# Another order of the q, k and gate projections, and a last norm whose root comes straight from the sum of squares

## The chip, the cores and the metric

The kernel runs on one core of one Trainium2 chip. The metric is the device time of one execution in microseconds. TensorE (PE, with PEld for its weight loads) does the matmuls, VectorE (DVE) and ScalarE (ACT) the elementwise work, and SyncE's queue (SP) issues nearly all transfers.

## The reference

One layer of a hybrid encoder block on x of 1024 tokens by 1024 channels, in float32:

```python
h = x + 0.5 * SwiGLU_1(rmsnorm(x))                   # d_ff 2816
u = rmsnorm(h)
q, k, v, g_ret, p, gates = split(u @ w_in)           # 4 x 1024, 1024, 2048 columns
q = rotary(q); k = rotary(k) / 16                    # 4 heads of 256
ret = rmsnorm(retention(q, k, v)) * silu(g_ret)      # chunks of 64, decay per head
pool_out = pool_scale * (pool(p) @ pool_w)           # trailing means over 2, 4, 8, 16 tokens, minus p
gate = sigmoid(gates + gate_bias)
h = h + (gate[0] * (ret @ w_ret_up) + gate[1] * (pool_out @ w_pool_up)) @ w_out
h = h + 0.5 * SwiGLU_2(rmsnorm(h))
return rmsnorm(h)
```

## The kernel before

The stages follow one another: first feed-forward, the projections out of the second norm, retention with the pooled branch as filler between its units, the merge, the second feed-forward, and the last norm. Every float32 operand is split into a high and a low part, and a product is three matmuls (`mm3`, lines 178 to 180). A large product is a Strassen form with seven products instead of eight, so sums of weight blocks and of result blocks are made on DVE and ACT.

`projections()` runs `values()` for v and then 24 groups of 256 output channels: p0 to p3, the eight gate groups t0 to t7, and q, k, g for four heads each. `pairs()` takes two groups of the list `order` at a time. In a pair, the product P3 (`A[5]`, `B[5]`) is formed for both groups in common, by a second Strassen level of 42 matmuls of 256 columns in place of 2 x 12 of 512; after the first `some` pairs (the number that `pairs` gets) P2 is done in common in the same way, and in the first `some` pairs P2 is run for each group by itself (`A[4]`, `B[4]`).

What follows a group is set by its kind in `end()`: a q or k group is rotated on DVE (`rotate`, with the tables cos and sin made by the first rotation) and stored; a t group goes through a sigmoid on ACT with a bias column, a g group through a silu on ACT, both then stored; a p group goes through `window`, which doubles trailing sums (line 1203) on DVE, finishes the mean and stores it. These pieces are put in the queue `flow.back`. In the projections one of them is taken off after each step of seven products (`flow.rate = 1`), so what a pair leaves behind is done beside the matmuls of the next one.

A result has the tiles A and B of a group (q3A and q3B of q3). They come from a pool of nine tiles of 128x1024 (`t4`), which also holds the window sums and cos and sin; a tile is free again when the store that reads it has landed. Raw weights come in four tiles (k3ra, k3rb of k3), split weights (k3wL, k3wS) in five. PSUM has eight banks; a bank is free when DVE or ACT has emptied it. In the common product the copies at lines 563, 566 and 583 empty banks into A of one of the two groups.

Retention works in units (head, half of the tokens). A unit's q, k, v are loaded, scores s are made, scaled by the decay (sc), split (sm), k is scaled (kd) and the state st is formed. `pool(n)` is the filler: it loads the pooled tiles (pl) and the pool weight (pw), splits them and runs eight groups of three matmuls into px, which ACT and DVE empty and split into po.

At the end, `Last` is the final norm. `gains` loads its gain row (n4row), and for each of four blocks of tokens `finish` takes the sum of squares of the second half of the row (n4q), adds what is known of the first half (n4e, `self.sums`), refines one over the root by one Newton step, and scales both halves.

Of the kernel before, what the change touches and what calls it, by code (L numbers as in the profile page):

```python
# [13 lines left out]
AF = mybir.ActivationFunctionType  # L14
ALU = mybir.AluOpType
ADD, SUB, MUL = ALU.add, ALU.subtract, ALU.mult
# [3 lines left out]
D = 1024  # L20
# [30 lines left out]
N_MV, N_T4, N_RAW, N_WT, N_TL, N_C2 = 28, 9, 4, 5, 4, 8  # L51
# [39 lines left out]
def block_kernel(ctx: ExitStack, tc, x, x_tok, vecs, f1_in, f1_out, w_in, w_v, pool_w, w_ret, w_pool, w_o,  # L91
                 f2_in, f2_out, g_row, rope, decay, consts, out, out_tok):
    nc = tc.nc
    mm = nc.tensor.matmul
    tt = nc.vector.tensor_tensor
    stt = nc.vector.scalar_tensor_tensor
    act = nc.scalar.activation
# [34 lines left out]
    def sum_bank(name):  # L132

        return ps.tile([P, H], F32, tag="sum", bufs=N_SUM, name=name)

    def load(dst, src):
        nc.sync.dma_start(dst, src)

    def eights(name):

        return sb.tile([P, 32], F32, tag="ss", bufs=2, name=name)[:, :8]
# [4 lines left out]
    def half(t, j):  # L146
        return t[:, j * H : (j + 1) * H]
# [49 lines left out]
    for n in range(N_SUM):  # L197
        b = sum_bank(f"set{n}")
# [68 lines left out]
    class Next(Norm):  # L267
# [22 lines left out]
        def g(self, mt, v=None):  # L290
            if self.gain is None:
                return None
            v = vec if v is None else v
            return v[:, self.gain + mt : self.gain + mt + 1]
# [297 lines left out]
    def pairs(nx, groups, some, tags, last):  # L592

        groups = list(groups)
        for n in range(0, len(groups), 2):
            both = n >= 2 * some
            A, B = (g((2, 3) if both else (3,)) for g in groups[n : n + 2])
            yield A[0]
            yield then(B[0], last) if n == len(groups) - 2 else B[0]
            if not both:  # L600
                yield A[4]
                yield then(B[4], nx.blocks("R21", tags, True)) if n == 2 * some - 2 else B[4]
            yield from (A[3], A[1], B[3], B[1], A[2], B[2])
            yield from common(nx, A, B, 2 if both else 3)
            yield A[6]
            yield B[6]
            if both:
                yield from common(nx, A, B, 3)

    def then(step, work):  # L610


        def body():
            step[1]()
            flow.add(*work)

        return step[0], body
# [484 lines left out]
    mix = Next("n2", V_MIX, h1)  # L1102
# [230 lines left out]
        yield from product("L12", "R21", "b", True, result(0, 0, lambda i: p1s.pop(i)))  # L1333
        yield from product("L22", "T4", "a", False, result(1, 0))

    order = [o for n, p in enumerate((1, 3, 2, 0)) for o in (("p", p), ("t", n))]
    order += [o for n in range(2) for kind in "qk" for o in ((kind, n), ("t", 4 + 2 * n + "qk".index(kind)))]
    order += [("q", 2), ("k", 2), ("q", 3), ("g", 0), ("k", 3), ("g", 1), ("g", 2), ("g", 3)]

    def projections():  # L1340
        yield from values()
        flow.rate = 1
        yield from pairs(mix, (project(*o) for o in order), 4, [("tl", N_TL), ("t4", N_T4), ("t4", N_T4)],
                         [units[0].loads])
        flow.rate = 2

# [76 lines left out]
    class Unit:  # L1423
# [141 lines left out]
        def finish(self):  # L1565
            for i in range(2):
                await_stored(f"g{self.h}")
                g = tl(f"rg{self.h}{i}")
                load(g, gs[2 * self.h + i])
                for nh in range(2):  # L1570
                    b = bank(f"ot{self.h}{nh}{i}")
                    for t in range(4):
                        o = t * HD + i * P
                        nc.tensor.transpose(b[:, t * P : (t + 1) * P], self.O[nh][:, o : o + P], ident)
                    tt(half(g, nh), b, half(g, nh), MUL)
                load(ret[2 * self.h + i], g)
# [153 lines left out]
    class Last(Norm):  # L1730
# [15 lines left out]
        def turned(self, acc):  # L1746


            def gains():
                self.row = sb.tile([P, S], F32, tag="mv", bufs=N_MV, name=f"{self.name}row")  # L1750
                load(self.row, g_row)
                self.ssq_e = eights(f"{self.name}sse")

            def done(n):

                o = self.rows[n] = sb.tile([P, S], F32, tag="mv", bufs=N_MV, name=f"{self.name}o{n}")
                b = self.turn([acc[mt] for mt in range(4)], n)
                act(half(o, 1), b, AF.Square, accum_out=self.ssq_e[:, n : n + 1])
                tt(half(o, 0), b, half(self.row, 0), MUL)
                v = self.sums[n] = sb.tile([P, 8], F32, tag="st", bufs=10, name=f"{self.name}e{n}")[:, :1]  # L1760
                nc.vector.tensor_scalar(v, self.ssq_e[:, n : n + 1], 1.0 / D, EPS, MUL, ADD)

            def rest(n):

                b = self.turn([acc[mt] for mt in range(4, 8)], n)
                if n < N_SUM:
                    self.banks[n] = sum_bank(f"{self.name}s{n}")
                    copy(self.banks[n], b)
                else:
                    copy(half(self.rows[n], 1), b)  # L1770

            return gains, *(lambda f=f, n=n: f(n) for n in range(4) for f in (done, rest))
# [9 lines left out]
        def finish(self, n):  # L1782
            o, b = self.rows[n], self.banks[n]

            def st(k):
                return sb.tile([P, 8], F32, tag="st", bufs=10, name=f"{self.name}{k}{n}")[:, :1]

            ss, v, r0, r1, t = st("q"), st("v"), st("r0"), st("r1"), st("t")
            with soon():
                act(half(o, 1), b, AF.Square, accum_out=ss)  # L1790
                nc.vector.tensor_scalar(v, ss, 1.0 / D, self.sums[n], MUL, ADD)
                r = self.root(v, r0, r1, t)
                stt(half(o, 1), b, r, half(self.row, 1), MUL, MUL)
                act(half(o, 0), half(o, 0), AF.Copy, scale=r)
                nc.scalar.dma_start(out_tok[n, :, :H], half(o, 0))
                load(out_tok[n, :, H:], half(o, 1))

        def root(self, v, r0, r1, t):

            act(r0, v, AF.Sqrt)  # L1800
            nc.vector.reciprocal(r1, r0)
            tt(t, r1, v, MUL)
            stt(t, t, -0.5, r1, MUL, MUL)
            stt(r0, t, 1.5, r1, ADD, MUL)
            return r0

        def end(self, part):
            if part != 3:
# [17 lines left out]
    def second():  # L1826
        for n, step in enumerate(ffn_in(ffn2, f2_in, ops2, "c")):
            flow.rate = 1
            yield step
        flow.rate = 2  # L1830
    flow.run(chain(ffn1(), projections(), retention(), merge(), second(),
                   ffn_out(ffn2, ops2, ops_done.setdefault("c", set()), f2_out, h2, "d", fin.quarter, fin.end, fin)))
    flow.some(-1)
# [86 lines left out]
```

## Time and profile before

| | us |
|---|---|
| median of 3 runs | 2155.76 (2154.02 to 2157.71) |
| profiled execution, own time | 2155.91 |
| its span, first to last instruction | 2154.1 |
| TensorE busy | 2138.4 (99%) |
| DVE busy | 1888.1 (88%) |
| ACT busy | 1109.4 (52%) |
| granted TensorE clock, mean | 0.999 |

The time is that of the profiled execution or of the runs; the span leaves out what lies before the first and after the last instruction. A busy share of an engine is a mean over stages. DMA rows give the time from a transfer's issue to its landing.

### The profile page before, as it was taken

How to read it: one execution, taken by the hardware profiler on the slowest of the kernel's cores; microseconds unless marked ns; L12 is line 12 of the kernel's file. 1: busy time of each engine (PE TensorE's matmuls, PEld its weight loads, DVE VectorE, ACT ScalarE, POOL GpSimd, SP SyncE). 2: the span in 40 equal slices, each digit the busy share in tenths (PEclk: the TensorE clock that was granted, in tenths of full speed). 3: DMA queues.
4: the chain of work that ended last, by engine and by line, in shares of the span. 5: the costliest groups of instructions: out<-in, count | busy, mean ns of one | idle time of the engine just before them, and what ended most of it. 6: DMA issues, size and time to landing. Idle time of an engine off the chain costs nothing.

```text
span 2154.1 us, 30246 instructions
## 1 busy us (share of the span) xinstructions
PE 2138.4 (99%) x10848; PEld 1816.3 (84%) x10848; DVE 1888.1 (88%) x3358; ACT 1109.4 (52%) x2106; POOL 0.2 (0%) x4
## 2 busy tenths in 40 slices
PE   9999999999999999999999999999999999999998
PEld 7888888888887888888888898887888888888887
DVE  8798888997987799999999877899988878899796
ACT  8544444454653544545456754446644544445454
POOL 0000000000000000000000000000000000000000
PEclk9999999999999999999999999999999999999999
DMA  7232423585537233332336567634123232358642
GB/s 256 76 133 74 138 83 128 181 289 180 185 117 241 89 118 116 120 137 98 108 119 234 179 221 259 219 97 158 68 97 123 74 132 90 127 181 292 197 131 99
DMA packets 120135, 320.96 MB, mean 149 GB/s; under 512 B 13232, under 2 KB 17456, under 8 KB 119984
## 3 DMA queue, kind: packets, MB, share of 16 engines
q1 hardware_dynamic: 119408, 317.98, 43.3%
q8 instruction: 85, 1.39, 0.3%
q10 hardware_dynamic: 576, 1.05, 0.1%
q14 instruction: 66, 0.54, 0.1%
HBM read 228.27 MB, written 90.70 MB: 148 GB/s over the span
## 4 chain that ended last, share of the span: by engine, by line
PE 87%; DVE 8%; DMA 2%; ACT 2%; issue 1%; SPq 0%; DVEq 0%; ACTq 0%
PE c_b L178 2%; PE c_b L180 2%; PE c_b L179 2%; PE a_b L178 2%; PE a_b L179 2%; PE a_b L180 2%; PE c_e L178 2%; PE c_e L179 2%; PE c_e L180 2%; PE a_e L179 2%; PE a_e L178 2%; PE a_e L180 2%; PE a_a L178 1%; PE a_a L179 1%; PE a_a L180 1%; PE c_a L179 1%
## 5 line engine op out<-in xcount | busy, mean ns | idle before, releaser
L179 PE MATMUL c_b<-n3T,c_wS 128*128 128x512 f32 x176 | 68.5, 389 | 0.0
L180 PE MATMUL c_b<-n3T,c_wS 128*128 128x512 f32 x176 | 68.5, 389 | 0.0
L178 PE MATMUL c_b<-n3T,c_wS 128*128 128x512 f32 x176 | 68.2, 389 | 0.0
L178 PE MATMUL a_b<-n1T,a_wS 128*128 128x512 f32 x168 | 65.4, 389 | 0.0
L179 PE MATMUL a_b<-n1T,a_wS 128*128 128x512 f32 x168 | 65.4, 389 | 0.0
L180 PE MATMUL a_b<-n1T,a_wS 128*128 128x512 f32 x168 | 65.3, 389 | 0.0
L179 PE MATMUL a_a<-n1R,a_wL 128*128 128x512 f32 x120 | 46.7, 389 | 0.0
L178 PE MATMUL a_a<-n1R,a_wL 128*128 128x512 f32 x120 | 46.7, 389 | 0.0
L180 PE MATMUL a_a<-n1R,a_wL 128*128 128x512 f32 x120 | 46.7, 389 | 0.0
L179 PE MATMUL c_a<-n3R,c_wL 128*128 128x512 f32 x112 | 43.7, 390 | 0.0
L178 PE MATMUL c_a<-n3R,c_wL 128*128 128x512 f32 x112 | 43.6, 389 | 0.0
L180 PE MATMUL c_a<-n3R,c_wL 128*128 128x512 f32 x112 | 43.6, 389 | 0.0
L180 PEld LDWEIGHTS c_b<-n3T,c_wS 128*128 128x128 f32 x176 | 33.0, 188 | 6.9
L179 PEld LDWEIGHTS c_b<-n3T,c_wS 128*128 128x128 f32 x176 | 33.0, 188 | 6.8
L178 PEld LDWEIGHTS c_b<-n3T,c_wS 128*128 128x128 f32 x176 | 33.0, 188 | 6.8
L159 DVE TENSOR_TENSOR a_wS<-a_S,a_wS 128x512 fp32r<-128x512 f32 x45 | 30.7, 683 | 8.9 <-ACT a_wS L158 8.9
L178 PEld LDWEIGHTS a_b<-n1T,a_wS 128*128 128x128 f32 x168 | 31.5, 188 | 6.6
L179 PEld LDWEIGHTS a_b<-n1T,a_wS 128*128 128x128 f32 x168 | 31.5, 188 | 6.5
L180 PEld LDWEIGHTS a_b<-n1T,a_wS 128*128 128x128 f32 x168 | 31.5, 188 | 6.5
L159 DVE TENSOR_TENSOR c_wS<-c_S,c_wS 128x512 fp32r<-128x512 f32 x46 | 31.4, 683 | 3.7 <-ACT c_wS L158 3.7
L179 PE MATMUL c_e<-n3T,c_wL 128*128 128x512 f32 x88 | 34.4, 391 | 0.0
L178 PE MATMUL c_e<-n3T,c_wL 128*128 128x512 f32 x88 | 34.4, 391 | 0.0
(3414 smaller groups left out, 8190.7 us busy)
## 6 DMA issues: line engine op xcount, KB each, us to landing
c_ra<-in_f_in SPq DMA_DIRECT2D x22, 512.0 KB, 3.7
c_rb<-in_f_in SPq DMA_DIRECT2D x22, 512.0 KB, 4.3
a_ra<-in_f_in SPq DMA_DIRECT2D x21, 512.0 KB, 3.7
a_rb<-in_f_in SPq DMA_DIRECT2D x21, 512.0 KB, 4.3
t<-au SPq DMA_DIRECT2D x11, 512.0 KB, 4.1
b<-ag SPq DMA_DIRECT2D x11, 512.0 KB, 3.5
r<-au SPq DMA_DIRECT2D x11, 512.0 KB, 3.8
br<-r SPq DMA_DIRECT2D x11, 512.0 KB, 5.3
```

The costliest lines, as they stand in the source:

```text
L159: tt(lo, src, hi.bitcast(F32), SUB)
L178: mm(dst, w[0], m[0], start=start, stop=False, skip_group_check=True)
L179: mm(dst, w[0], m[1], start=False, stop=False, skip_group_check=True)
L180: mm(dst, w[1], m[0], start=False, stop=stop, skip_group_check=True)
```

## The change

In `order`, (q0,k0) becomes the first pair, ahead of the four pairs of a p and a t. Behind it the q and k of the other heads and the remaining t and g follow pairwise:

| | pairs in order |
|---|---|
| before | (p1,t0) (p3,t1) (p2,t2) (p0,t3), then (q0,t4) (k0,t5) (q1,t6) (k1,t7) (q2,k2) (q3,g0) (k3,g1) (g2,g3) |
| after | (q0,k0) (p1,t0) (p3,t1) (p2,t2) (p0,t3), then (q1,t4) (k1,t5) (q2,t6) (k2,t7) (q3,g0) (k3,g1) (g2,g3) |

In the pairs ahead of "then" only P3 is formed in common; `some` goes from 4 to 5. In the last norm the gain row is scaled by -0.5 on ACT after its load; the root is taken on ACT straight from the sum of squares, with its scale and with the first half's part as bias, beside the making of v on DVE; and the step for one over the root ends in (t - 3) x r1, whose factor -0.5 is the gain row's.

```diff
-    order = [o for n, p in enumerate((1, 3, 2, 0)) for o in (("p", p), ("t", n))]
-    order += [o for n in range(2) for kind in "qk" for o in ((kind, n), ("t", 4 + 2 * n + "qk".index(kind)))]
-    order += [("q", 2), ("k", 2), ("q", 3), ("g", 0), ("k", 3), ("g", 1), ("g", 2), ("g", 3)]
+    light = [("t", n) for n in range(8)] + [("g", n) for n in range(4)]
+    heavy = [("p", n) for n in (1, 3, 2, 0)] + [(kind, n) for n in range(1, 4) for kind in "qk"]
+    order = [("q", 0), ("k", 0), *(o for pair in zip(heavy, light) for o in pair), *light[len(heavy) :]]
...
-        yield from pairs(mix, (project(*o) for o in order), 4, [("tl", N_TL), ("t4", N_T4), ("t4", N_T4)],
+        yield from pairs(mix, (project(*o) for o in order), 5, [("tl", N_TL), ("t4", N_T4), ("t4", N_T4)],
...
                 load(self.row, g_row)
+                act(self.row, self.row, AF.Copy, scale=-0.5)
...
                 act(half(o, 1), b, AF.Square, accum_out=ss)
+                act(r0, ss, AF.Sqrt, scale=1.0 / D, bias=self.sums[n])
                 nc.vector.tensor_scalar(v, ss, 1.0 / D, self.sums[n], MUL, ADD)
-                r = self.root(v, r0, r1, t)
-                stt(half(o, 1), b, r, half(self.row, 1), MUL, MUL)
-                act(half(o, 0), half(o, 0), AF.Copy, scale=r)
+                nc.vector.reciprocal(r1, r0)
+                stt(t, r1, v, r1, MUL, MUL)
+                stt(r0, t, -3.0, r1, ADD, MUL)
+                stt(half(o, 1), b, r0, half(self.row, 1), MUL, MUL)
+                act(half(o, 0), half(o, 0), AF.Copy, scale=r0)
...
-        def root(self, v, r0, r1, t):
-
-            act(r0, v, AF.Sqrt)
-            nc.vector.reciprocal(r1, r0)
-            tt(t, r1, v, MUL)
-            stt(t, t, -0.5, r1, MUL, MUL)
-            stt(r0, t, 1.5, r1, ADD, MUL)
-            return r0
```

On ACT, in the pair (q3,g0), with the weights of the next pair (k3wL, k3wS, g1wL), the copies into q3A and g0A, and the silu of g0B with its table load. Before:

```order
L158 CAST q3wy_10148<-g0S_9915 128x256
L1183 ACT_TABLE_LOAD
L1183 ACTIVATE g0B<-g0B 128x1024
L158 CAST k3wL_10170<-k3ra 128x512
L158 CAST g1wL_10191<-g1ra 128x512
L158 CAST k3wS_10219<-k3rb 128x512
L566 COPY g0A<-q3y_10073 128x256
```

After:

```order
L158 CAST q3wy_10111<-g0S_9890 128x256
L158 CAST k3wL_10131<-k3ra 128x512
L563 COPY q3A<-q3x_10155 128x256
L566 COPY g0A<-q3y_10156 128x256
L1183 ACT_TABLE_LOAD
L1183 ACTIVATE g0B<-g0B 128x1024
L158 CAST g1wL_10152<-g1ra 128x512
```

The cast of k3wL and the copy L566 have moved ahead of the table load and the silu, and a copy L563 stands between them.

On SP, at the step from the projections to retention, with the stores of the g groups (from g2B, g3B, g2A, g3A), the loads of q and k of the next unit and of the second pool weight (pw). Before:

```order
L137 DMA g_205<-g2B 128x1024
L137 DMA g_207<-g3B 128x1024
L137 DMA q_11004<-q_184 128x512
L137 DMA q_11004<-q_185 128x512
L137 DMA k_11007<-k_192 128x512
L137 DMA g_204<-g2A 128x1024
L137 DMA k_11007<-k_193 128x512
L137 DMA g_206<-g3A 128x1024
L137 DMA pw_11072<-in_pool_w 128x512
```

After:

```order
L137 DMA g_205<-g2B 128x1024
L137 DMA pw_11033<-in_pool_w 128x512
L137 DMA q_10965<-q_184 128x512
L137 DMA g_207<-g3B 128x1024
L137 DMA q_10965<-q_185 128x512
L137 DMA k_10968<-k_192 128x512
L137 DMA g_204<-g2A 128x1024
L137 DMA k_10968<-k_193 128x512
L137 DMA g_206<-g3A 128x1024
```

The load of pw has moved from behind the store of g3A to behind the store of g2B, ahead of three stores.

On DVE in the same place, from g3A's last step to the first part of kd (v, sc, pl, sm, pw, po, kd as in the section before). Before:

```order
L1485 TENSOR_TENSOR sc_11051<-s_11038,dec_10802 128x256
L159 TENSOR_TENSOR pl_11058<-pl_11056,pl_11058 128x512
L159 TENSOR_TENSOR sm_11035<-sc_11033,sm_11035 128x512
L159 TENSOR_TENSOR sm_11053<-sc_11051,sm_11053 128x256
L159 TENSOR_TENSOR pl_11061<-pl_11056,pl_11061 128x512
L159 TENSOR_TENSOR pl_11066<-pl_11064,pl_11066 128x512
L163 SCALAR_TENSOR_TENSOR po_11111<-px_11097,vec,po_11111 128x512
L163 SCALAR_TENSOR_TENSOR po_11114<-px_11098,vec,po_11114 128x512
L159 TENSOR_TENSOR pl_11069<-pl_11064,pl_11069 128x512
L159 TENSOR_TENSOR pw_11074<-pw_11072,pw_11074 128x512
L163 SCALAR_TENSOR_TENSOR po_11131<-px_11117,vec,po_11131 128x512
```

After:

```order
L159 TENSOR_TENSOR sm_10996<-sc_10994,sm_10996 128x512
L159 TENSOR_TENSOR pl_11022<-pl_11017,pl_11022 128x512
L159 TENSOR_TENSOR sm_11014<-sc_11012,sm_11014 128x256
L159 TENSOR_TENSOR pl_11027<-pl_11025,pl_11027 128x512
L159 TENSOR_TENSOR pl_11030<-pl_11025,pl_11030 128x512
L159 TENSOR_TENSOR pw_11035<-pw_11033,pw_11035 128x512
L163 SCALAR_TENSOR_TENSOR po_11072<-px_11058,vec,po_11072 128x512
L163 SCALAR_TENSOR_TENSOR po_11075<-px_11059,vec,po_11075 128x512
L163 SCALAR_TENSOR_TENSOR kd_11039<-kd00b_11038,cst,kd_11039 128x256
L163 SCALAR_TENSOR_TENSOR kd_11049<-kd00b_11048,cst,kd_11049 128x256
L163 SCALAR_TENSOR_TENSOR po_11092<-px_11078,vec,po_11092 128x512
```

The last pl and the pw have moved ahead of the first two po, and two kd ahead of the third po.

## The prediction

> **What bounds the kernel now.** I read the page's first part, then the waits of the matmul engine, then its busy time by stretches, and last the timelines around the stretches that fall short.
>
> ```profile
> span 2154.1 us, 30246 instructions
> PE 2138.4 (99%) x10848; PEld 1816.3 (84%) x10848; DVE 1888.1 (88%) x3358; ACT 1109.4 (52%) x2106; POOL 0.2 (0%) x4
> ```
>
> TensorE is busy for 99% of the span, so time comes off in two ways only: fewer or cheaper matmuls, or closing one of the few holes between them. DVE's 88% is the next engine; it matters where DVE's demand in one pair of projections comes near the pair's matmul time. The waits of PE (us in total, times, longest) name the holes:
>
> ```profile
> PE k3a L178 <- ACT g0A L566: 1.6, 1, 1.6
> PE ob L178 <- DVE po L163: 1.6, 1, 1.6
> PE st L180 <- DVE kd L163: 0.5, 1, 0.5
> PE t4e L180 <- DVE t4wS L159: 0.4, 1, 0.4
> ```
>
> The first lies at the end of the projections, the second at the start of retention; both are stretches whose instructions the change moves. By stretches (start:end, length, then busy us of PE, PEld, DVE, ACT, POOL, the granted clock, the DMA share):
>
> ```profile
> 780.00:817.00 37.00, 37.00 (x184) 31.35 (x183) 35.83 (x58) 16.62 (x37) 0.00 (x0) 1.00 0.33 114
> 1004.00:1041.00 37.00, 37.00 (x207) 32.24 (x206) 33.92 (x63) 17.91 (x32) 0.00 (x0) 1.00 0.33 115
> 1078.00:1115.00 37.00, 35.38 (x198) 30.65 (x198) 35.57 (x65) 19.05 (x35) 0.00 (x0) 1.00 0.35 127
> 1175.00:1180.00 5.00, 3.71 (x18) 3.71 (x19) 5.00 (x11) 4.22 (x10) 0.00 (x0) 0.66 0.68 261
> ```
>
> A pair of a q or k with a gate (second row) and a pooled pair (first row) keep PE full; the pair (q3,g0) loses 1.62 us, and the retention start loses time twice, by a hole and by a clock of 0.66.
>
> **The change, part by part.**
>
> *Matmuls.* The diff raises the number of leading pairs with P3 alone in common from four to five, so one more pair runs its own P2: 24 matmuls of 512 columns take the place of 42 of 256. Start to start in the timeline of PE:
>
> ```profile
> 1084.91 0.28 PE L180 MATMUL q3b<-n2R,q3ws 128*128 128x256 f32 x1
> 1085.03 0.28 PE L178 MATMUL q3b<-n2R,q3ws 128*128 128x256 f32 x1
> ...
> 1171.72 0.39 PE L178 MATMUL px<-pl,pw 128*128 128x512 f32 x1
> 1171.95 0.39 PE L179 MATMUL px<-pl,pw 128*128 128x512 f32 x1
> ```
>
> Over longer stretches these steps average 0.114 and 0.227 us, so 24 x 0.227 - 42 x 0.114 = **+0.66 us** on the bound engine, with no cover.
>
> *The hole at k3a.*
>
> ```profile
> 1083.38 0.69 DVE L1173 TENSOR_TENSOR k2B<-k2B,k2c 128x512 f32<-128x512 f32 x1
> ...
> 1083.61 1.28 ACT L1183 ACT_TABLE_LOAD   x1
> 1084.90 1.06 ACT L1183 ACTIVATE g0B<-g0B 128x1024 f32<-128x1024 f32 x1
> 1085.88 0.60 ACT L158 CAST k3wL<-k3ra 128x512 fp32r<-128x512 f32 x1
> ...
> 1087.42 0.63 ACT L566 COPY g0A<-q3y 128x256 f32<-128x256 f32 x2
> ...
> 1085.93 0.28 PE L180 MATMUL g0b<-n2R22y,q3wy 128*128 128x256 f32 x1
> 1087.83 0.50 PE L178 MATMUL k3a<-n2R,k3wL 128*128 128x512 f32 x1 [1.62 <-ACT g0A L566]
> ...
> k<-k2B SPq DMA_DIRECT2D x1, 512.0 KB, 2.6
> ```
>
> PE needs the PSUM bank that the copy L566 empties into a t4 tile. That tile was k2B's; it comes free only when k2B's store has landed, 2.6 us after an issue that follows the rotation's last step (1083.38 + 0.69): 1086.7. The pair (q2,k2) carries two rotations, so DVE's rotation work ran into the next pair; and ACT stood in the table load and the silu. After the change two rotations share a pair only in (q0,k0), and the pair after it, (p1,t0), has no window's steps to run beside them yet; (q2,t6), (k2,t7) and (q3,g0) are like the steady pair of the second row, with 37.00 of 37.00. ACT runs the two copies ahead of the table load. Step to step the hole is 1.90, less a normal 0.11, and the next matmul steps add 0.12: **-1.9 us**. Bounds: 0 (the wait stays) and -2.2. I take -1.9, since what follows next, DVE's 33.9 us in 37, is not late anywhere in the steady rows.
>
> *Retention's start.*
>
> ```profile
> 1168.56 0.96 SPq L137 DMA_DIRECT2D pw<-in_pool_w  x1
> ...
> 1173.57 0.62 ACT L158 CAST pw<-pw 128x512 fp32r<-128x512 f32 x1 [2.67 <-DMA pw<-in_pool_w]
> 1174.10 1.26 ACT L162 ACTIVATE po<-px,vec 128x512 fp32r<-128x512 f32 x2
> ...
> 1166.93 0.87 DVE L163 SCALAR_TENSOR_TENSOR v<-v,n2r,v 128x256 fp32r<-128x256 f32 x2
> ...
> 1172.64 0.28 PE L178 MATMUL st<-v,kd 128*128 128x256 f32 x1
> ...
> 1174.25 0.49 PE L178 MATMUL px<-pl,pw 128*128 128x512 f32 x1
> 1176.29 0.58 PE L178 MATMUL ob<-v,sm 128*128 128x256 f32 x1 [1.55 <-DVE po L163]
> ...
> 1179.80 0.28 PE L178 MATMUL st<-v,kd 128*128 128x256 f32 x1
> 1179.92 0.28 PE L179 MATMUL st<-v,kd 128*128 128x256 f32 x1
> ```
>
> The second pool weight is loaded behind the store of g3A, ACT waits 2.67 us for it with the last two po behind it, and so the bank for ob is late. The hole is 2.04 us from px to ob where a step is 0.23 (1.8), 0.2 more ahead of px, and then half clock: the 16 matmuls of 256 from 1176.29 to 1179.80 take 3.51 us where the pitch of the last two rows (0.12) makes it 1.92 (1.6). Together 3.6 us. After the change the load is issued ahead of the last q and g stores and its cast stands ahead of the last two silus. That wait is gone, and DVE's queue is what is late next: the third st matmul needs kd, which stands behind g3A's last step and then v, two sc, four pl, two sm, pw and two po, twelve steps. From 1166.93, where that v starts now, these take, by the steps between starts in this trace (about 0.6 for a 128x512, five of them and one sm; 0.66 for a po; 0.35 to 0.5 for the four smaller), 0.6 x 6 + 0.66 x 2 + 1.7 = 6.6 us, and kd itself 0.4: 1173.9 to 1174.4 with the waits between, while PE is there at 1172.64. A new wait of 1.3 to 1.8 us replaces the old one. If the clock stays up that saves about 2.1 us, if it drops for the same stretch 0.5; with everything gone it saves 3.6, with everything kept 0. I take **-1.5 us**, between the two first.
>
> Two holes of the same length speak on the clock: after 1.62 us at k3a the next stretch shows 1.00 in this row, after 1.55 us at ob it shows 0.66 in the row above.
>
> ```profile
> 1085.00:1090.00 5.00, 3.38 (x24) 2.95 (x23) 4.79 (x10) 3.05 (x7) 0.00 (x0) 1.00 0.49 202
> ```
>
> So a wait of this length can go either way. The Trainium skill (TensorE: Matmul & The Clock Gate, Part 1, "What's actually happening") has the clock halve only after an idle window of about 3.4 us; by that rule neither hole would cost clock, and removing the one at ob would be worth its 2.0 us alone, so the sum would come out nearer 2154.0 with a new wait of 1.5 us in its place. The 0.66 behind a 1.55 us hole disagrees with it, and the measurement decides.
>
> *A new tightness.* cos and sin are loaded by the first rotation and kept. They hold two of the nine t4 tiles, now through the pooled pairs as well, where before they were not there until the pooled pairs were over. The windows' doubling steps (L1203) take a t4 tile each and wait for a store to land:
>
> ```profile
> gt<-t2A SPq DMA_DIRECT2D x1, 512.0 KB, 2.6
> ```
>
> In a pooled pair DVE is busy 35.83 of 37.00, so it has 1.17 us to give before PE sees anything. By the order of the queue I find the stores in time by 0.3 to 1.2 us in the tightest pair. Bounds 0 and +3; I take **+0.2 us**.
>
> *The tail.*
>
> ```profile
> 2148.14 0.20 ACT L1790 ACTIVATION_READ_ACCUMULATOR n4o<-dp5a 128x1 f32 x1
> 2148.36 0.21 DVE L1791 TENSOR_SCALAR n4v<-n4q,n4e 128x1 f32<-128x1 f32 x1 [5.46 <-ACT n4o L1790]
> 2148.61 0.20 ACT L1800 ACTIVATE n4r<-n4v 128x1 f32<-128x1 f32 x1 [0.28 <-DVE n4v L1791]
> 2148.85 0.16 DVE L1801 RECIPROCAL n4r<-n4r 128x1 f32<-128x1 f32 x1 [0.27 <-ACT n4r L1800]
> 2149.04 0.16 DVE L1802 TENSOR_TENSOR n4t<-n4r,n4v 128x1 f32<-128x1 f32 x1
> ```
>
> Of the four finishes only the last is behind the last matmul. v leaves the path (2148.36 to 2148.61, -0.25), and one of three refining steps goes (2148.85 to 2149.04, -0.2). The root now reads its bias from a tile (+0.1, the difference of the gates' sigmoid with a bias tile, 1.16, and the silu, 1.06), and a step reads v as a pointer (+0.05, a scalar step with a pointer 0.21 against 0.16). Sum **-0.30 us**, bounds -0.1 and -0.45.
>
> ```profile
> L1190 ACT ACTIVATE t0B<-t0B,vec x1: 1155/1155/1155, 754.9 to 754.9; 128x1024 f32<-128x1024 f32 x1
> ...
> ACT dp5w L158 <- PE dp5a L180: 10.6, 6, 2.1
> ```
>
> The gain row's multiply on ACT (about 1.06 us like a silu) stands in the second feed-forward's weight casts, where ACT idles up to 2.1 us ahead of each dp5w; 1.06 fits, so nothing. Without that cover it would be 1.06.
>
> **The sum** against the profiled execution's own time, 2155.91: +0.66 - 1.9 - 1.5 + 0.2 - 0.30 = -2.84, which gives 2153.07. The median of the runs before is 2155.76, 0.15 lower, so the median forecast is **2152.9**.
>
> **Rivals.** *A, retention's start loses nothing.* DVE reaches kd by 1172.6, because some of the twelve steps ahead of it (the four pl and the pw, whose loads and casts now start earlier) are done before 1166.9. For it: what these wait for is there sooner, and the 2.67 us that ACT waits now is free for the casts. Against it: the queue's order, by which all twelve come behind g3A's last step.  It saves 3.6 instead of 1.5: 2150.8, faster. Chance 0.25.
>
> *B, the t4 tiles run short (slower).* In the three pairs that run the windows of p1, p3 and p2 each doubling step waits for the store of the gate before it. One wait of 2.6 us per pair less DVE's 1.17 costs 1.4, two cost 4.0; the middle, 2.7, three times is +8.1. From 2152.9 - 0.2 that is 2160.8. It decides from the point where the store of t0A lands after DVE comes to the first step of p1's window. For it: DVE's small slack; against it: the 2.6 us landing is short against a pair of 37. Chance 0.12.
>
> *C, the change does not do what it says at k3a*: the hole was made by the table load of 1.28 us and the silu, and that pair of instructions still stands in this pair, now ahead of g1wL. Then 1.28 of the 1.9 comes back: 2154.2. Chance 0.1. *D, the clock drops again behind the new wait*: -0.5 instead of -1.5, 2153.9. Chance 0.13. The forecast as it stands: 0.40.
>
> **How the numbers follow.** 0.2% is 4.3 us, about what a measurement of this kernel can tell from no change (the three runs before span 3.7). Faster by that is below 2151.4, slower above 2160.1. A falls below with 0.21 of its 0.25 (with a smaller k3a gain it doesn't), the forecast with 0.11 of its 0.40 by the low bounds of its terms: 0.32. B's upper part gives 0.08 and an unforeseen hole of the same kind in the new pair at the start 0.02: 0.10. The rest, 0.58, is within. The range: the low end takes all low bounds, -2.2, -3.6, -0.45, 0 and +0.66, -5.6 from 2155.76, which is 2150.2, and 0.5 for waits that I count as staying (t4e): 2149.7. The high end is B with one wait per pair (2152.7 + 4.2): 2156.9. What lies outside is B's upper part and part of A.
>
> **What would show it.** Right: 1041 to 1115 shows no wait of k3a on L566; PE's waits name st or ob at retention with 1 to 2 us; from the accumulator read to the step that scales the last tile about 0.3 us less pass; PE's busy time loses nothing in the four pooled pairs. Wrong: a wait of a window's step (L1203) on a store that passes to PE; a wait of PE in (q0,k0) on cos or sin; the k3a wait kept with the table load as its releaser; a granted clock of 0.66 in more than one stretch of 5 us.

## The result and the profile after

The median of 22 runs is 2152.94 us (2150.44 to 2155.07) against 2155.89 (22 runs) of the kernel before; the ratio is 0.9985, 95% interval 0.9979 to 0.9991, so 1.9 to 4.5 us less. The profiled execution of the changed kernel took 2153.71, against 2155.91 before: 2.20 less.

The page's first lines, and the waits of PE (us in total, times, longest):

```profile
span 2151.9 us, 30188 instructions
PE 2136.8 (99%) x10830; PEld 1814.0 (84%) x10830; DVE 1884.0 (88%) x3344; ACT 1110.4 (52%) x2102; POOL 0.2 (0%) x4
```

```profile
PE st L180 <- DVE kd L163: 1.2, 2, 0.7
...
PE ru1b L180 <- DVE ru1wS L159: 0.7, 1, 0.7
...
PE t4e L180 <- DVE t4wS L159: 0.4, 1, 0.4
```

The waits of k3a and of ob are gone. In their place stands one more wait of st on kd, 0.7 us long, at retention's start; t4e has stayed. The wait of ru1b is in the merge, where the change moved no instruction.

Where the 2.20 us went is read from four places in PE's timeline: the first matmul of the pairs of groups in the projections (p1a before, q0a after; v's products come ahead of them), the first scores (s), the first matmul of the pooled branch's second step (pu1d), and the last matmul. Before:

```profile
713.53 0.39 PE L178 MATMUL p1a<-n2R,p1wL 128*128 128x512 f32 x1
...
1163.31 0.28 PE L178 MATMUL s<-q,k 128*128 128x256 f32 x1
...
1235.51 0.48 PE L692 MATMUL pu1d<-po,pu1w 128*128 128x512 f32 x1
...
2147.22 0.39 PE L180 MATMUL dp5a<-dp4w,dp4m 128*128 128x512 f32 x1
```

After:

```profile
713.61 0.39 PE L178 MATMUL q0a<-n2R,q0wL 128*128 128x512 f32 x1
...
1161.95 0.28 PE L178 MATMUL s<-q,k 128*128 128x256 f32 x1
...
1232.09 0.48 PE L692 MATMUL pu1d<-po,pu1w 128*128 128x512 f32 x1
...
2145.28 0.39 PE L180 MATMUL dp5a<-dp4w,dp4m 128*128 128x512 f32 x1
```

| stage, us | before | after | difference |
|---|---|---|---|
| projections, first matmul to first s | 449.78 | 448.34 | -1.44 |
| first s to first pu1d | 72.20 | 70.14 | -2.06 |
| first pu1d to last matmul | 911.71 | 913.19 | +1.48 |
| last matmul to end of span | 6.9 | 6.6 | -0.29 |

The first matmul of the pairs starts 0.08 later than before, and rounding makes the rest. In the third stage the order of the matmuls is as before; 0.97 of its +1.48 lies in the merge, with the wait of ru1b, and 0.50 in the second feed-forward. The second feed-forward takes from 612.6 to 614.6 us in the traces of all runs, so its 0.50 is scatter. The wait of ru1b is not: the three traces with `some = 5` (the changed kernel, e1 and e8 below) have a gap of 0.8 to 1.3 us there (matmul start to start, less the usual step), in both orders, and of the eleven with 4 or 6 only e7 has a part of it, 0.35. So it goes with the number five, and about 1 us is a price of the change in a stage that it didn't touch; by what path is not shown.

The tail, from the accumulator read on:

```profile
2146.20 0.20 ACT L1791 ACTIVATION_READ_ACCUMULATOR n4o<-dp5a 128x1 f32 x1
2146.43 0.29 ACT L1792 ACTIVATE n4r<-n4q,n4e 128x1 f32<-128x1 f32 x1
2146.43 0.21 DVE L1793 TENSOR_SCALAR n4v<-n4q,n4e 128x1 f32<-128x1 f32 x1 [5.75 <-ACT n4o L1791]
2146.76 0.16 DVE L1794 RECIPROCAL n4r<-n4r 128x1 f32<-128x1 f32 x1
2146.96 0.22 DVE L1795 SCALAR_TENSOR_TENSOR n4t<-n4r,n4v 128x1 f32<-128x1 f32 x1
2147.21 0.16 DVE L1796 SCALAR_TENSOR_TENSOR n4r<-n4t,n4r 128x1 f32<-128x1 f32 x1
2147.41 0.72 ACT L1798 ACTIVATE n4o<-n4o,n4r 128x512 f32<-128x512 f32 x1 [0.68 <-DVE n4r L1796]
```

From the read to the scaling step 1.21 us pass (2147.41 - 2146.20), where it was 1.49. The root and v start together, the root takes 0.29 with its bias from a tile instead of 0.20.

### The profile page after: what moved, and what is told of

Same layout as the page of the kernel before. It is cut to its first block, busy times and chain, and to the rows that moved or that the text cites. A ratio compares the mean times of both kernels' runs of the same rounds, so it can differ in the third digit from the quotient of the medians.

```text
span 2151.9 us, 30188 instructions
## 1 busy us (share of the span) xinstructions
PE 2136.8 (99%) x10830; PEld 1814.0 (84%) x10830; DVE 1884.0 (88%) x3344; ACT 1110.4 (52%) x2102; POOL 0.2 (0%) x4
## 4 chain that ended last, share of the span: by engine, by line
PE 83%; DVE 11%; DMA 2%; ACT 2%; issue 2%; SPq 0%; DVEq 0%; ACTq 0%
PE c_b L178 2%; PE c_b L179 2%; PE c_b L180 2%; PE a_b L178 2%; PE a_b L180 2%; PE a_b L179 2%; PE c_e L178 2%; PE c_e L179 2%; PE c_e L180 2%; PE a_e L179 2%; PE a_e L180 2%; PE a_e L178 2%; PE a_a L180 1%; PE a_a L179 1%; PE a_a L178 1%
## 5 line engine op out<-in xcount | busy, mean ns | idle before, releaser
L179 PE MATMUL c_e<-n3T,c_wL 128*128 128x512 f32 x88 | 34.4, 391 | 0.0
L178 PE MATMUL c_e<-n3T,c_wS 128*128 128x512 f32 x88 | 34.4, 391 | 0.0
```

What stands on the lines that cost most here:

```text
L178: mm(dst, w[0], m[0], start=start, stop=False, skip_group_check=True)
L179: mm(dst, w[0], m[1], start=False, stop=False, skip_group_check=True)
```

## The experiments

A gap is told here too as the distance between two matmul starts less the usual step.

**e1, e2: the two halves of the change.** e1 has the new `order` and `some = 5` with the old norm; e2 the new norm with the old order and `some = 4`.

> The new order with five pairs, the norm as before. Theory (order and norm add up, and the norm is worth its 0.3 us of the tail): about 2.6 us under the kernel before, no PE wait on L566 of 1.6 us, no clock under 1.00 at retention's start, and from the last matmul to the span's end 6.9 us as before. Rival (the gain is mostly the norm's, or holes elsewhere that come and go): within 1 us of the kernel before.

> The new norm with the old order and four pairs. Theory: 0.3 us under the kernel before, which the rounds can't tell from zero; in the trace 6.6 us from the last matmul to the span's end instead of 6.9, and the waits of k3a (1.6) and ob (1.6) still there. Rival (the gain row's step on ACT disturbs the last feed-forward): a wait near 2041 us and a time up to 1 us over the kernel before.

e1: ratio 0.9988 (0.9979 to 0.9997), about 2.6 us less; projections 448.40, first s to first pu1d 70.15, as in the changed kernel, and the old tail of 6.9. e2: 0.9995 (0.9987 to 1.0004), not to be told from no change; in its trace the tail is 6.6 and both waits are there. The order makes most of the gain, and the parts add up within the intervals.

```profile
PE k3a L178 <- ACT g0A L566: 1.6, 1, 1.6
PE ob L178 <- DVE po L163: 1.5, 2, 1.3
```

Those are e2's waits of PE. But its first s to first pu1d took 70.60, not 72.20: see the clock, below.

**e3: the new order with four pairs.**

```diff
-        yield from pairs(mix, ..., 5, [...]
+        yield from pairs(mix, ..., 4, [...]
```

> The changed kernel, but four pairs with P3 alone in common instead of five: the pair (p0,t3) forms P2 in common too. Theory (matmul time is what bounds, P2 alone costs 0.66 us): 0.66 us under the changed kernel and PE busy 0.7 us less in that stretch. Rival (the pooled pair needs the longer matmul time to cover DVE, 35.8 us of 37): a new wait of PE of 1 to 2 us on DVE in (p0,t3), and a time 0.5 to 1.5 us over the changed kernel.

2163.02 us, ratio 1.0029 (1.0018 to 1.0040): 6.3 us slower than before, and ten over the changed kernel, which neither the theory nor the rival had. The fifth pair with its own P2 is what the new order needs. Its waits of PE and timeline of ACT, with SP's issue of t3B's store:

```profile
PE p0x L178 <- ACT p0A L563: 3.4, 1, 3.4
```

```profile
897.60 0.33 SPq L137 DMA_DIRECT2D gt<-t3B  x1
...
900.21 0.19 ACT L1204 COPY p2s<-p2s 128x4 f32<-128x4 f32 x1 [0.22 <-DMA gt<-t3B]
902.28 0.65 ACT L563 COPY p0A<-p0x 128x256 f32<-128x256 f32 x2 [1.88 <-DVE p2s L1203]
```

This is the chain of rival B in another place: the window of p2 takes a t4 tile that t3B still holds; t3B's store lands 2.6 us after its issue; the window's copy on ACT waits for it; the copy that empties PSUM stands behind that copy and waits 1.88 us more, for the window's doubling step on DVE; and PE waits 3.4 us. The second-level sums of R21, which are made ahead of the first pair that shares P2, hold two t4 tiles, as the call's list of tags says; with cos and sin four of nine are then held while p2's window still needs its own.

**e9: e3 with one table for cos and sin**, so with one t4 tile more:

```diff
-        for n, z in (("cos", 0), ("sin", 1)):
-            tab[n] = t4(n)
-            load(tab[n], rope[z])
-            tt(tab[n], tab[n], mix.rms(), MUL)
+        tab["cos"] = tab["sin"] = t4("cos")
+        load(tab["cos"], rope[0])
+        tt(tab["cos"], tab["cos"], mix.rms(), MUL)
```

> The new order with four pairs, as in the run with four before, but the rotation uses one table for cos and sin (a part of the computation is changed), so one t4 tile is free that the run with four lacked. Theory (the pooled pairs run short of t4 tiles, since cos and sin and the two tiles of the second-level sums are held while p0 and p2 still need theirs): the wait of p0x of 3.4 us is gone or under 0.5, the half clock behind it too, and the time is 6 to 9 us under that run, 0 to 2 us under the changed kernel. Rival (DVE's work, 37.00 of 37.00 there, or the shorter matmul time is what is missing): a wait of 2 us or more stays in (p0,t3), and the time stays 4 us or more over the changed kernel; DVE's own saving is one table step of 1.2 us.

2157.05, ratio 1.0006 (0.9997 to 1.0015): by the ratios about 5 us under e3 and 4.5 over the changed kernel. So about half of e3's loss goes with one tile more (and with one step less on DVE, which this edit also saves), and half stays, as the rival had it. The wait for the store is gone, but another has come in the same pair:

```profile
PE p0y L178 <- ACT p0ws L158: 3.6, 1, 3.6
```

```profile
902.91 0.62 ACT L158 CAST p0ws<-p0s 128x512 fp32r<-128x512 f32 x1 [1.57 <-DVE p0s L540]
```

```profile
865.00:902.00 37.00, 34.89 (x179) 29.34 (x177) 37.00 (x68) 18.15 (x41) 0.00 (x0) 1.00 0.33 114
```

DVE is busy 37.00 of 37.00 us in e9 up to the hole (last row, by stretches): the sums of weights for the next products come after the pair's results and the window. The clock drops behind this hole too, to 0.70 and 0.62 in the two stretches of 5 us from 900 on. So the tiles explain part of e3's loss; that DVE's load in (p0,t3) makes the rest is read from the trace, and no run tests it.

**e4: no pair with two rotations, and no pair moved ahead.** The kernel before with another last line of `order`:

```diff
-    order += [("q", 2), ("k", 2), ("q", 3), ("g", 0), ("k", 3), ("g", 1), ("g", 2), ("g", 3)]
+    order += [("q", 2), ("g", 0), ("k", 2), ("g", 1), ("q", 3), ("g", 2), ("k", 3), ("g", 3)]
```

> The kernel before with its four pairs, but (q2,g0) (k2,g1) (q3,g2) (k3,g3) at the end in place of (q2,k2) (q3,g0) (k3,g1) (g2,g3): no pair has two rotations, and no pair is moved ahead. Theory (the hole at k3a comes from two rotations in one pair, and the price of the fifth pair isn't needed): the k3a hole is gone, 1.9 us under the kernel before by that alone; the last pair's rotation of k3 now runs into retention, which costs DVE up to 2.5 us there, so the time is 0 to 2 us under the kernel before. Rival (the hole comes from the table load of the first silu): a hole of about 1.3 us in (q2,g0) or right behind it.

2159.58, ratio 1.0013 (1.0004 to 1.0021): 2.8 us slower, a miss of the expected 0 to 2 us less. The hole at k3a is gone, and none is by the table load; the projections take 449.61 all the same, since a wait of k3x has come in the last pair. And from the first s to the first pu1d it takes 75.10 us, 2.9 more than before, with DVE rotating k3 there:

```profile
PE k3x L178 <- DVE k3A L573: 1.0, 1, 1.0
```

```profile
1171.67 0.68 DVE L1173 TENSOR_TENSOR k3B<-k3B,k3c 128x512 f32<-128x512 f32 x1
1172.28 1.40 DVE L163 SCALAR_TENSOR_TENSOR po<-px,vec,po 128x512 fp32r<-128x512 f32 x2
```

This order pays in retention for ending with a rotation. With the last pair free of one, the twelve p, q and k groups stand in eleven pairs, so one pair holds two of them; the change puts that pair at the front.

**e5, e6: what makes the hole at k3a.** e5 takes the table load away (the silu of the g groups becomes a sigmoid), e6 takes k2's rotation out; both on the kernel before.

```diff
-            act(pair[i], pair[i], AF.Silu)
+            act(pair[i], pair[i], AF.Sigmoid)
```

```diff
-                flow.add(*rotate(0), *rotate(1), lambda: keep(qs if kind == "q" else ks))
+                turns = () if name == "k2" else (*rotate(0), *rotate(1))
+                flow.add(*turns, lambda: keep(qs if kind == "q" else ks))
```

> The kernel before, with a sigmoid in place of the silu of the g groups (part of the computation is changed): the table load of 1.28 us ahead of g0B's activation goes, and the order on every engine stays. If the hole at k3a were set by k2B's store alone, it stays at 1.8 us. If it were set by ACT's row of work ahead of the copy L566 alone, it shrinks by 1.28 to 0.5. If by both, the copy starts when the store lands, 1084.09 + 2.6 = 1086.7 instead of 1087.42, and it shrinks by 0.7 to 1.1. The time falls by as much, 0 to 1.3 us.

> The kernel before, with k2 stored as it is (its rotation is left out, so one rotation stays in the pair (q2,k2)); the table load and the silu stay. Theory (the second rotation makes k2's tiles late, and that sets the hole and ACT's order): no wait of k3a over 0.2 us, ACT does the copies ahead of the table load, and the time is 2 us under the kernel before. Rival (the table load and the silu make the hole): a hole of 1.3 us or more stays in (q3,g0).

e5: the gap at k3a falls from 1.79 to 1.19, by 0.6; the time is not to be told from before (1.0005, 0.9996 to 1.0015; other holes in its trace were larger, one of 0.74 at g2x among them). PE in e5:

```profile
1086.29 0.28 PE L180 MATMUL g0b<-n2R22y,q3wy 128*128 128x256 f32 x1
1087.59 0.50 PE L178 MATMUL k3a<-n2R,k3wL 128*128 128x512 f32 x1 [1.02 <-ACT g0A L566]
```

And ACT in e5, ahead of the copy that k3a waits for:

```profile
1086.64 0.62 ACT L158 CAST k3wS<-k3rb 128x512 fp32r<-128x512 f32 x1 [0.70 <-PE g0b L180]
1087.17 0.64 ACT L566 COPY g0A<-q3y 128x256 f32<-128x256 f32 x2
```

The store alone (no change) is not it. The fall of 0.6 is near the 0.7 of store and row together, but it doesn't show the store: with the table load gone, ACT's row has a gap of its own, 0.70 us for PE ahead of the cast of k3wS, and the copy stands right behind that cast. So e5 shows ACT's row in the hole and leaves the store open. e6: ratio 0.9988 (0.9978 to 0.9997), about 2.6 us less; no wait of k3a, with the table load and the silu still there, behind the two copies:

```profile
1082.47 0.62 ACT L158 CAST k3wL<-k3ra 128x512 fp32r<-128x512 f32 x1 [0.43 <-ACT q3wy L158]
1083.13 0.37 ACT L563 COPY q3A<-q3x 128x256 f32<-128x256 f32 x1
1083.81 0.37 ACT L566 COPY g0A<-q3y 128x256 f32<-128x256 f32 x1 [0.31 <-PE q3y L180]
1084.20 1.28 ACT L1183 ACT_TABLE_LOAD   x1
```

And more came with it: from the first s to the first pu1d e6 takes 70.11, as the changed kernel does, with the wait of st on kd in place of that of ob. So retention's start was not a second cause: both gains follow from one pair without its second rotation, late in the projections.

**e7: the pool weights on another queue**, on the kernel before:

```diff
-            load(half(r, 0), pool_w[n])
+            nc.gpsimd.dma_start(half(r, 0), pool_w[n])
```

> The kernel before, with the loads of the pool weights issued by GpSimd's queue, so that they stand behind no store. Theory (the hole at ob comes from the load of the second pool weight behind g3A's store): ACT's wait of 2.67 us for pw is gone and the hole at ob is under 0.5 us, with a new wait of up to 1.5 us at st as in the changed kernel; the time is 0.5 to 2 us under the kernel before. Rival (the load waits for its buffer): pw lands about 1173.5 as before and the hole stays.

2158.38, ratio 1.0017 (1.0008 to 1.0026): 3.7 us slower, against the theory. The rival has a part: on a queue with nothing ahead of it the load still waited for its buffer, until DVE's step of pl was done, as the first row below names it. It was issued at 1162.79, and its cast now stands on ACT ahead of g3A's silu and waits for it:

```profile
1162.79 0.54 POOL L1360 DMA_DIRECT2D pw<-in_pool_w  x1 [12.40 <-DVE pl L159]
...
1168.93 0.62 ACT L158 CAST pw<-pw 128x512 fp32r<-128x512 f32 x1 [3.69 <-DMA pw<-in_pool_w]
1169.46 1.05 ACT L1183 ACTIVATE g3A<-g3A 128x1024 f32<-128x1024 f32 x1
```

A load that is issued earlier but used earlier still gains nothing here: everything behind the cast on ACT is late, and PE's waits of ob grow from 1.6 to 3.3. In the changed kernel the cast has moved ahead as well, but there the load is issued at 1158.77, four us earlier, and the cast waits 0.92 instead of 3.69.

**e8, e10: one more pair with P2 by itself.** e8 is the kernel before with `some = 5`, e10 the changed kernel with `some = 6`.

> The kernel before in its own order, but with five pairs that have P3 alone in common: (q0,t4) runs P2 by itself. Theory (P2 alone costs matmul time only): TensorE is busy 0.66 us longer in that pair and the holes at k3a and ob are as before, so 0.7 us over the kernel before. Rival (the work on weight sums for the second level, moved by one pair away from the windows of the pooled groups, frees DVE): the wait of t4e (0.4) goes and the time is as before or under it. Also seen here, in a part that is unchanged: whether the clock drops behind the hole at ob in each execution (0.66 in a 5 us stretch) or in some.

> The changed kernel with six pairs that have P3 alone in common: (q1,t4) runs P2 by itself too. Theory (from the run of the old order with five, where the wait of t4e went with it): the wait of t4e (0.6) goes, P2 costs 0.66, so within 0.5 us of the changed kernel. Rival (matmul time only): 0.7 us over it.

e8: 1.0008 (0.9999 to 1.0018), not to be told from no change. The wait of t4e is gone, a gap of 0.96 at q2x has come, and the projections take 450.22. e10: 2153.19, ratio 0.9991 (0.9982 to 1.0001) to the kernel before; projections 447.59, 0.75 less than the changed kernel in spite of the added matmul time, with no wait of t4e; by the intervals it cannot be told from the changed kernel. P2 alone costs its 0.66 us, but a gap of 0.6 at t4e goes where t4's pair is no longer the first to share it.

**e11, e12: the clock behind the hole at ob.** The kernel before and e2's kernel, unchanged, once more.

> The kernel before, unchanged, for one more look at the clock behind the hole at ob. If the drop belongs to the place, the 4 us behind the hole show 0.57 to 0.7 again and lose 1.4 to 1.6 us; if it comes and goes, 1.00 in some. The hole itself is 1.8 either way, and the one at k3a shows 1.00 behind it.

> The new norm with the old order, once more, for the same look: its first execution showed a hole of 1.5 us at ob and a clock of 1.00 behind it. If the shorter hole is the reason, a hole of 1.8 here goes with a dropped clock, one of 1.5 with 1.00; if it is chance, either goes with either.

Both show a gap of 1.82 at ob and a dropped clock behind it; in e11 the drop begins later, so that 1178 to 1182 shows 0.58. The stretch of 1176 to 1180 us in the kernel before, in e2, e11 and e12, one row of each (the clock is the third number from the end):

```profile
1176.00:1180.00 4.00, 3.71 (x18) 3.71 (x19) 4.00 (x10) 3.22 (x8) 0.00 (x0) 0.57 0.64 246
```

```profile
1176.00:1180.00 4.00, 3.71 (x30) 3.67 (x31) 4.00 (x11) 4.00 (x10) 0.00 (x0) 1.00 0.74 255
```

```profile
1176.00:1180.00 4.00, 3.06 (x18) 3.06 (x19) 4.00 (x11) 3.86 (x10) 0.00 (x0) 0.74 0.67 248
```

```profile
1176.00:1180.00 4.00, 3.13 (x15) 3.13 (x16) 4.00 (x11) 3.79 (x9) 0.00 (x0) 0.57 0.68 268
```

Of the seven profiled executions with a hole at ob (before, e2, e5, e7, e8, e11, e12) six dropped the clock; e2, with a gap of 1.5, did not. The seven holes at k3a (1.2 in e5, 1.8 in the others) had 1.00 behind them each time, as had the new hole of 0.9 at st in the changed kernel, e1 and e6. What tells ob from k3a stays open: the two are as long. One difference stands in the traces and was not tested: with a drop, the hole at ob and the gaps of 0.2 or more within 3 us ahead of it come to 2.0 us or more (1.82 and 0.21 before), while the hole at k3a is alone with 1.8, and e2's two gaps come to 1.8.

## Why the prediction was right, and where its steps were not

The forecast of 2152.9 stands beside 2152.94, and that nearness is luck. The projections and retention's start gave 0.96 us more than their terms, and the third stage took 1.48 back, for which the sum has no term: about 1 of it is the merge's new wait of ru1b, the rest scatter. In the profiled execution, from which the terms were read, 2153.71 stands against 2153.07. What was right is the kind of the gain: two holes smaller or gone, and a shorter tail.

*The tail:* -0.30 forecast, -0.29 in the table of stages, by the steps named: the root's hop, one refining step, 0.09 for the bias from a tile.

*k3a:* -1.9 forecast. The gap is gone; the pair's stretch keeps PE full now, where 35.38 was:

```profile
1078.00:1115.00 37.00, 37.00 (x206) 32.23 (x205) 34.47 (x63) 18.87 (x34) 0.00 (x0) 1.00 0.34 115
```

With +0.66 for P2 and +0.2 for the tight pair the forecast for the projections was -1.04; -1.44 was measured. By the steps between matmul starts P2 costs its 0.66 and the hole gives its 1.9; the 0.2 for the tight pair did not come, and 0.2 more came off in many steps of under 0.1 each. The reason given for the hole was half of it. The prediction had the store of k2B set the copy's start (1086.7); the copy began only at 1087.42, when ACT had done the table load, the silu and three casts. e5 shows that row in the hole, and leaves open whether the store has a part. What e6 shows is the common root: the second rotation. Rival C, in which the table load makes the hole wherever it stands, fell with e4 and e6, though by e5 0.6 of the hole hung on it.

*Retention's start:* -1.5 forecast, -2.06 measured. The new wait is at st for kd, as forecast, but 0.9 us long instead of 1.3 to 1.8. The steps from DVE's v behind g3A's last step to kd take 6.6 us as worked out:

```profile
1165.06 0.47 DVE L163 SCALAR_TENSOR_TENSOR v<-v,n2r,v 128x256 fp32r<-128x256 f32 x1
...
1171.65 0.86 DVE L163 SCALAR_TENSOR_TENSOR kd<-kd00b,cst,kd 128x256 fp32r<-128x256 f32 x2
...
1171.17 0.28 PE L179 MATMUL st<-v,kd 128*128 128x256 f32 x1
1172.18 0.39 PE L180 MATMUL st<-v,kd 128*128 128x256 f32 x1 [0.73 <-DVE kd L163]
```

What was wrong is where they begin: that v starts 1.87 us earlier than before (1165.06 for 1166.93) and PE comes to that st 1.36 earlier (1171.28, a step of 0.11 behind 1171.17, for 1172.64), so DVE gains 0.5 on PE that the step did not have. The larger part of the difference is the clock. The two middle cases were 2.1 with the clock up and 0.5 with it dropped; it stayed up. Against e2, in which the clock had stayed up before as well, the stage gains only 0.46 us (70.60 to 70.14); against the others 2.06 to 2.67 (72.20 of before, 72.81 of e11, 72.70 of e12). The drop can be priced: the same 16 matmuls from ob on take 3.51 us before, as the prediction read them, and 2.01 in e2:

```profile
1176.29 0.38 PE L178 MATMUL ob<-v,sm 128*128 128x256 f32 x1 [1.34 <-DVE po L163]
...
1178.30 0.28 PE L178 MATMUL st<-v,kd 128*128 128x256 f32 x1
```

So about three quarters of this gain, 1.5 of 2.06, are a clock drop that no longer happens. That the 2.06 meets the 2.1 of the case with the clock up is luck again: the wait is 0.4 to 0.9 shorter than in that case, but the steps right behind it are 0.37 longer than usual, and a gap of 0.36 has come at a later s, which the kernel before doesn't have:

```profile
1186.63 0.38 PE L180 MATMUL s<-q,k 128*128 128x256 f32 x1 [0.19 <-DVE k L159]
```

By the rule of the Trainium skill that the prediction weighed (TensorE: Matmul & The Clock Gate, Part 1, "What's actually happening": the clock halves after an idle window of about 3.4 us) the clock's part of this gain could not be. A clock of 0.57 to 0.74 behind gaps of 1.8 us in three executions disagrees with it as it was read; the 1.00 behind the gaps of 1.8 at k3a agrees.

*The t4 tiles:* +0.2 forecast; the changed kernel shows no wait of that kind, with DVE at 36.87 and 36.78 of 37 in two of the pooled pairs. Rival B was not the case here, but e3 met its mechanism with two more tiles held, at 6.3 us over the kernel before, to which DVE's load adds.

```profile
750.00:787.00 37.00, 37.00 (x185) 31.44 (x184) 36.87 (x64) 13.51 (x25) 0.00 (x0) 1.00 0.27 91
861.00:898.00 37.00, 37.00 (x186) 31.44 (x185) 36.78 (x65) 17.68 (x38) 0.00 (x0) 1.00 0.30 107
```

*The gain row:* nothing, as forecast; the multiply takes 1.06 us on ACT and no wait of PE names it. Rival A, no loss at all at retention's start, did not come: 0.9 us is left.

## What to carry to other kernels

When the matmul engine is full, look for the stretch in which the next engine has two large pieces of follow-up work at once, and move one of them to where follow-up work is light; here that took two holes away, of which only one looked related. Before such a move, count the buffers that its tables and sums hold while others still need theirs: in the same order, with one pair fewer that runs P2 by itself, the gain of 3 us became a loss of 6, about half of which one more tile took back. When a transfer is issued earlier and its consumer moves ahead too, compare the two moves: with the load at 1158.77 the cast waited 0.92 us in its new place, with the load at 1162.79 it waited 3.69 and held back all that ACT had behind it. And add up all the stages, those that the change leaves alone too: here a stage behind the change took back about 1 us, and the agreement of the total hid it.

## What the hardware showed that was not expected

A gap of 1.8 us between matmuls was followed by a clock of 0.57 to 0.74 over about 4 us at one place and by 1.00 at another, with the same outcome in nearly every execution; a hole of 3.5 us in e3 was followed by 0.70, 0.50 and 0.78 in three stretches of 5 us, with a smaller gap of 1.3 in the second:

```profile
900.00:905.00 5.00, 2.29 (x10) 2.30 (x11) 4.19 (x7) 1.45 (x4) 0.00 (x0) 0.70 0.00 2
905.00:910.00 5.00, 4.02 (x15) 3.34 (x15) 3.85 (x7) 1.27 (x5) 0.00 (x0) 0.50 0.26 105
910.00:915.00 5.00, 5.00 (x21) 4.29 (x21) 4.34 (x8) 2.98 (x7) 0.00 (x0) 0.78 0.00 0
```
